# One-hot factors of the PEER gate matrix: built for 12 tokens at once in bf16, with the gate in three bf16 parts

## The chip, the cores and the metric

The kernel runs on one core of one Trainium2 chip. The metric is the device time of one execution in microseconds (us), as the median over runs; lower is better. Three runs of the kernel before gave 2867.94, 2873.04 and 2873.58 us.

## The reference

The program is a whole two-layer model in fp32 on 512 tokens of width 1024: a mixing layer (HGRN2 and retention branches), a PEER feed-forward layer, and a second block with recurrent, stick-breaking and differential attention and a gated feed-forward. Only the PEER layer is touched here. It retrieves, for each token and each of 8 heads, 16 of 16384 experts, and adds their outputs:

```python
s = jnp.einsum('thpd,hpkd->thpk', q, sub_keys.astype(jnp.float32))
top_s, top_i = lax.top_k(s, PEER_TOPK)
cand = top_s[:, :, 0, :, None] + top_s[:, :, 1, None, :]
cand_idx = top_i[:, :, 0, :, None] * PEER_NKEYS + top_i[:, :, 1, None, :]
...
gates = jax.nn.softmax(best_s, axis=-1)
...
act = jax.nn.gelu(jnp.einsum('td,thkd->thk', xb, u).astype(jnp.float32))
w = (gb * act).astype(xb.dtype)
return jnp.einsum('thk,thkd->td', w, v)
```

An expert's number is 128·i + j, with i and j below 128. So the gates of one token can be written as a 128x128 matrix G with G[j, i] the summed gate of expert (i, j): the product of a matrix of 128 selections by a one-hot of j, and one of 128 selections by a one-hot of i scaled with the gate.

## The kernel before

For tokens 0 to 383 (`SD = 384`, three tiles of 128) the kernel doesn't gather experts. It computes the activation of all 16384 experts densely, builds G for every token, and multiplies. For tokens 384 to 511 it gathers the rows of the chosen experts by indirect DMA, a fixed number per step (`gathers`, function `gath`); VectorE takes a product and sum of each gathered tile (line 1050, tile `junk`).

The dense part goes in steps. A step `u_step` (line 795) handles 256 experts. `begin` fetches the weights of later steps (SyncE's queue) and writes their high parts (`whi`, ScalarE, line 74). Then come the callbacks: `early`, `finish_split` (the low parts `wlo`, VectorE, line 79), `pre` (gathers and selection work), two `u_block`s on TensorE (line 779; 8 x 3 matmuls of 384 columns each, lines 58 to 60), `mid`, two GELUs on ScalarE with the store of the result (lines 819, 821), and `post`.

In 32 of these steps (12 tokens each, `TS = 12`) G is built as well; I call them gate steps.

- `g_pre` (line 995), called in `early`: for each token it makes two fp32 tiles of 128x128. J is a one-hot of j. For 11 of the 12 tokens ScalarE makes it in two passes, `Abs(iota - j)` (line 1005) and `Relu(1 - .)` (line 1011); for one token VectorE does it (line 1003). I is the one-hot of i times the gate, one VectorE instruction a token (line 1006). The per-token numbers are columns of `iT`, `jT`, `gT`, which hold the transposed indices and gates with selections on the partitions.
- `g_mid` (line 1014), called in `mid`: one fp32 matmul a token (line 1019) into `sx`, four tokens in a bank of PSUM.
- `g_post` (line 1023), called in `post`: ScalarE copies four tokens into `gst` with the token innermost, 16 tokens apart (line 1029), and a DMA stores every 16 tokens (line 1031).

`transposes` (line 896) makes `iT`, `jT` and `gT` of one 128-token tile: three TensorE transposes (line 904) and three ScalarE copies (line 906). It is called at the end of `mid`, so those copies stand ahead of the step's GELUs in ScalarE's order. It acts three times.

The order of the work on each engine is that in which the code issues it (`manual_schedule`); a step's TensorE work is: 48 matmuls of 384 columns, then the step's gate matmuls. The tiles J and I have twelve buffers for twelve tokens, so those of a step reuse the buffers that the step before read.

Of the kernel before, what the change touches and what calls it, by code (L numbers as in the profile page):

```python
# [7 lines left out]
F32 = mybir.dt.float32  # L8
BF16 = mybir.dt.bfloat16
# [3 lines left out]
AF = mybir.ActivationFunctionType  # L13
ALU = mybir.AluOpType
# [3 lines left out]
P = 128  # L18
S = 512
NT = S // P  # L20
D = 1024
# [6 lines left out]
TS = 12  # L28
# [3 lines left out]
ND = 3  # L32
# [675 lines left out]
def peer(c):  # L708
    nc, d, W = c.nc, c.d, c.W
# [3 lines left out]
    def pool(name, **kw):  # L713
        cm[name], p = c.open(name, **kw)
        return p
# [8 lines left out]
    keep = pool("p_keep")  # L724
# [9 lines left out]
        close("p_n")  # L734
    gb = pool("p_gb", bufs=2)
    gc = pool("p_gc")
    iT = gc.tile([P, ND, P], F32, name="iT")
    jT = gc.tile([P, ND, P], F32, name="jT")
    gT = gc.tile([P, ND, P], F32, name="gT")
    iota = gc.tile([P, P], F32, name="iota")  # L740
    nc.scalar.dma_start(iota, d["c_iota"])
    se = pool("p_se", bufs=2, side="right")
    s1 = pool("p_s1", side="right")
    TV = s1.tile([P, NT, 4, 16], F32, name="TV")
# [142 lines left out]
    def finish(t):  # L887
        if t < ND:
            trans.append((2, t))
        else:  # L890
            ij = IJ[t].rearrange("p u a b -> p u (a b)")
            nc.vector.scalar_tensor_tensor(gI, ij[:, 0], float(P), ij[:, 1], op0=ALU.mult, op1=ALU.add)
            ready.add(t)

    def transposes():
        if trans:
            k, t = trans.pop(0)
            if k:
                trans.insert(0, (k - 1, t))
                return  # L900
            ij = IJ[t].rearrange("p u a b -> p u (a b)")
            pt = tr.tile([P, 3, P], F32, tag="tr", name="tr")
            for u, src in enumerate((ij[:, 0], ij[:, 1], ge[:, t].rearrange("p a b -> p (a b)"))):
                nc.tensor.transpose(pt[:, u, :], src, c.ident)
            for u, (dst, sgn) in enumerate(((iT, 1.0), (jT, -1.0), (gT, 1.0))):
                nc.scalar.activation(dst[:, t, :], pt[:, u, :], AF.Copy, scale=sgn)
            ready.add(t)

    def halves(sc, t, hp):
# [62 lines left out]

    IJ, wide = {}, {}

# [9 lines left out]
    def fold(t, u):  # L984
        oh = wide[t, u]
        if u == 0:
            IJ[t] = se.tile([P, 2, 8, 16], F32, tag="ij", name="ij")
        for n in (8, 4, 2):
            nc.vector.tensor_add(oh[:, :, :, :n], oh[:, :, :, :n], oh[:, :, :, n:2 * n])
        nc.vector.tensor_add(IJ[t][:, u], oh[:, :, :, 0], oh[:, :, :, 1])  # L990

    stage = [None]
    NJ = 1

    def g_pre(t0):
        IJ = []
        for tt in range(t0, t0 + TS):
            t, u = divmod(tt, P)
            J = gb.tile([P, P], F32, tag="J", bufs=TS, name="J")
            I = gb.tile([P, P], F32, tag="I", bufs=TS, name="I")  # L1000
            lone = (tt - t0) % 4 == 3 and (tt - t0) // 4 < NJ
            if lone:
                nc.vector.tensor_scalar(J, iota, jT[:, t, u:u + 1], 0.0, op0=ALU.add, op1=ALU.is_equal)
            else:
                nc.scalar.activation(J, iota, AF.Abs, bias=jT[:, t, u:u + 1])  # L1005
            nc.vector.tensor_scalar(I, iota, iT[:, t, u:u + 1], gT[:, t, u:u + 1],
                                    op0=ALU.is_equal, op1=ALU.mult)
            IJ.append((I, J))
            if len(IJ) % 4 == 0:
                for _, J in IJ[-4:len(IJ) - 1 if lone else None]:  # L1010
                    nc.scalar.activation(J, J, AF.Relu, bias=1.0, scale=-1.0)
        return IJ

    def g_mid(IJ):
        pgs = []
        for q in range(0, TS, 4):
            pg = sx.tile([P, 4, P], F32, tag="sx", name="sx")
            for u in range(4):
                nc.tensor.matmul(pg[:, u, :], IJ[q + u][1], IJ[q + u][0], start=True, stop=True)
            pgs.append(pg)  # L1020
        return pgs

# [10 lines left out]
    def gather(table, n):  # L1033
        rows = keep.tile([P, D], F32, tag="rows", bufs=4, name="rows")
        nc.gpsimd.indirect_dma_start(out=rows, out_offset=None, in_=table,  # L1035
                                     in_offset=bass.IndirectOffsetOnAxis(ap=gI[:, n:n + 1], axis=0))
        return rows

    def gath():
        q = []  # L1040
        for n in range(2 * P + 4 - 1):
            if n < 2 * P:
                q.append(gather(d["expert_u"] if n < P else d["expert_v"], n % P))
            if n < 4 - 1:
                continue
            m = n - 4 + 1
            rows = q[m]
            if m < P:
                junk = keep.tile([P, D], F32, tag="junk", bufs=2, name="junk")
                nc.vector.scalar_tensor_tensor(junk, rows, 1.0, hG, op0=ALU.mult, op1=ALU.mult,  # L1050
                                               accum_out=gA[:, m:m + 1])
                if m == P - 1:
                    nc.scalar.activation(gA, gA, AF.Gelu_apprx_tanh)
                    nc.vector.tensor_mul(gG, gG, gA)
            else:
                g = gG[:, m - P:m - P + 1]
                if m == P:
                    nc.vector.tensor_scalar(hG, rows, g, None, op0=ALU.mult)
                else:
                    o = c.xs[:, ND, :] if m % 2 else hG  # L1060
                    nc.vector.scalar_tensor_tensor(o, rows, g, o, op0=ALU.mult, op1=ALU.add)  # L1061
                if m == 2 * P - 1:
                    nc.vector.tensor_add(c.xs[:, ND, :], c.xs[:, ND, :], hG)
            done[0] += 1
            yield 1
# [10 lines left out]
    n = 1  # L1076
# [29 lines left out]
    def v_weight(k):  # L1106
        p = vsteps[k]
        a = acts[p // 2][:, 2 * (p % 2):2 * (p % 2) + 2, :]
        whi = vg[0].tile([P, 2, SD], F32R, tag="Whi", name="Whi")
        wlo = vg[0].tile([P, 2, SD], F32R, tag="Wlo", name="Wlo")  # L1110
        gv = Gt[p // 4].rearrange("p b i t -> p i b t")[:, 2 * (p % 4):2 * (p % 4) + 2]
        av = a.rearrange("p i (b t) -> p i b t", t=TB)
        nc.vector.tensor_mul(av, av, gv)
        nc.scalar.copy(whi, a)
        nc.vector.tensor_sub(wlo, a, whi)
        wt[k] = (whi, wlo)
# [10 lines left out]
    while order[n][0] == "u":  # L1127
        st = {}
        p = order[n][1]
        go = toks < SD and (toks + TS - 1) // P in ready  # L1130

        def early():
            if go:
                st["IJ"] = g_pre(toks)
            elif vg[0] is not None:
                if not wt and order[n + 2][0] == "v":
                    v_weight(0)
            else:
                work(1.5)

        def pre():
            if ND in ready:
                gathers(RATE_W if first or rest else RATE_G if go else RATE_U)
            work(1.5 if ND in ready else 3)

        def mid():
            if go:
                st["pg"] = g_mid(st["IJ"])
            transposes()

        def post():
            if go:
                g_post(toks, st["pg"])
        if len(ready) == NT and res[0] is None:
            close("p_s1", "p_se")
            if c.second:
                b_tables(c)
            res[0] = pool("p_res", side="right")
        u_step(n, p, early, pre, mid, post)
        if go:  # L1160
            toks += TS
        elif toks >= SD and vg[0] is None and order[n + 4][0] == "v":
            close("p_gc", "p_gb", "p_ub")
            vg[0] = pool("v_g", bufs=2)
            for k in range(4):
                v_fetch(k)
        n += 1
# [5 lines left out]
    for k in range(64):  # L1173
        begin(n)
        if k + 4 < 64:
            v_fetch(k + 4)
        if k + 1 < 64:
            v_weight(k + 1)
        w = finish_split(n)
        n += 1  # L1180
        gathers(RATE_V)
        if c.second and k == 50:
            wr = keep.tile([P, D], F32, tag="junk", bufs=2, name="row_final")
            row_load(c, wr, "final_norm_w")
        if k < 62:
            for j in range(2):
                for t in range(ND):
                    prods(k, j, t, w)
        elif k == 62:
            w62 = w  # L1190
# [168 lines left out]
def second(c, out):  # L1359
# [273 lines left out]
    def project(n):  # L1633
# [13 lines left out]
        else:  # L1647
            dv = tmaj(2304)
    sq = sk = sv = dq = dk = dv = None
    st = pxt[:, 1]  # L1650
    ops = dict(X=project, I=lru1, J=lru2, K=lru3, M=lru4, A=stick_a, B=stick_b, C=stick_c, D=stick_d, a=diff_a, b=diff_b,
               c=diff_c, d=diff_d, e=diff_e, Y=y_proj, S=splits, T=diff_T, t=lambda t: run(tile_t(0, t)),
# [258 lines left out]
```

## Time and profile before

| what | value |
|---|---|
| median of 3 runs (lowest to highest) | 2873.04 us (2867.94 to 2873.58) |
| span of the profiled execution | 2869.7 us |
| TensorE matmul (PE) busy | 2792.8 us, 97% |
| TensorE weight load (PEld) busy | 2454.2 us, 86% |
| VectorE (DVE) busy | 1876.6 us, 65% |
| ScalarE (ACT) busy | 1249.2 us, 44% |
| GpSimd (POOL) busy | 427.3 us, 15% |

The profiled execution comes with its span alone, from its first instruction to its last; no time around it is given, and the span lies 3.3 us below the median of the runs. The shares are means over the whole program, which has stages with different limits. The gate steps lie between 1197 and 1573 us of the span, an eighth of it, and what the change does has to be read there.

### The profile page before, as it was taken

How to read it: one execution, taken by the hardware profiler on the slowest of the kernel's cores; microseconds unless marked ns; L12 is line 12 of the kernel's file. 1: busy time of each engine (PE TensorE's matmuls, PEld its weight loads, DVE VectorE, ACT ScalarE, POOL GpSimd, SP SyncE). 2: the span in 40 equal slices, each digit the busy share in tenths (PEclk: the TensorE clock that was granted, in tenths of full speed). 3: DMA queues.
4: the chain of work that ended last, by engine and by line, in shares of the span. 5: the costliest groups of instructions: out<-in, count | busy, mean ns of one | idle time of the engine just before them, and what ended most of it. 6: DMA issues, size and time to landing. Idle time of an engine off the chain costs nothing.

```text
span 2869.7 us, 40522 instructions
## 1 busy us (share of the span) xinstructions
PE 2792.8 (97%) x15905; PEld 2454.2 (86%) x15905; DVE 1876.6 (65%) x3717; ACT 1249.2 (44%) x2110; POOL 427.3 (15%) x333
## 2 busy tenths in 40 slices
PE   8999999999999999999999999999999999999998
PEld 7888888988989889999999988888887766888988
DVE  4666434345453999967777677777777568575475
ACT  4222223322233325689999333333334676432232
POOL 0000011011000002323332433232331020010010
PEclk9999999999999999999999999999999999999999
DMA  4111222222233237889999889999993210322222
GB/s 144 69 65 59 74 96 78 92 83 77 77 118 96 100 107 263 280 305 324 334 325 331 319 296 330 334 333 336 340 347 131 83 59 30 82 91 89 100 86 77
DMA packets 177679, 499.18 MB, mean 174 GB/s; under 512 B 46288, under 2 KB 96080, under 8 KB 144208
## 3 DMA queue, kind: packets, MB, share of 16 engines
q1 hardware_dynamic: 94416, 311.16, 30.8%
q0 software_dynamic: 36864, 134.23, 13.2%
q10 hardware_dynamic: 46208, 51.18, 5.1%
q8 instruction: 126, 2.06, 0.3%
q14 instruction: 65, 0.53, 0.1%
HBM read 448.83 MB, written 47.71 MB: 173 GB/s over the span
## 4 chain that ended last, share of the span: by engine, by line
PE 76%; DVE 8%; ACT 7%; issue 4%; DMA 3%; ACTq 1%; POOL 1%; DVEq 0%; POOLq 0%
PE mm L58 15%; PE mm L60 15%; PE mm L59 15%; PE acc L60 6%; PE acc L59 6%; PE acc L58 6%; DMA rows<-expert_u,gI 2%; ACT J L1005 2%; PE ax L385 1%; ACT gst L1029 1%; ACT whi L74 1%; DVE wlo L79 1%; PE ax L59 1%; PE ax L58 1%; PE ax L60 1%
## 5 line engine op out<-in xcount | busy, mean ns | idle before, releaser
L79 DVE TENSOR_TENSOR wlo<-wraw,whi 128x2048 fp32r<-128x2048 f32 (+1 forms) x250 | 561.6, 2246 | 394.5 <-ACT whi L74 382.8
L58 PE MATMUL mm<-hh,whi 128*128 128x512 f32 (+2 forms) x2064 | 755.9, 366 | 14.1 <-ACT hh L244 7.3
L74 ACT CAST whi<-wraw 128x2048 fp32r<-128x2048 f32 (+1 forms) x250 | 468.7, 1875 | 683.9 <-PE acc L60 305.9
L60 PE MATMUL mm<-hh,wlo 128*128 128x512 f32 (+2 forms) x2064 | 747.3, 362 | 8.8 <-DVE wlo L79 8.3
L59 PE MATMUL mm<-hl,whi 128*128 128x512 f32 (+2 forms) x2064 | 748.3, 363 | 0.3
L58 PEld LDWEIGHTS mm<-hh,whi 128*128 128x128 f32 x2064 | 390.7, 189 | 57.6 <-ACT hh L244 8.4
L60 PEld LDWEIGHTS mm<-hh,wlo 128*128 128x128 f32 x2064 | 390.4, 189 | 53.1 <-DVE wlo L79 11.6
L59 PEld LDWEIGHTS mm<-hl,whi 128*128 128x128 f32 x2064 | 390.5, 189 | 41.7 <-DVE hl L245 1.1
L59 PE MATMUL acc<-wlo,Whi 128*128 128x512 f32 x768 | 304.6, 397 | 0.1
L58 PE MATMUL acc<-whi,Whi 128*128 128x512 f32 x768 | 304.5, 397 | 0.0
L60 PE MATMUL acc<-whi,Wlo 128*128 128x512 f32 x768 | 304.5, 396 | 0.0
L1035 POOL DMA_INDIRECT rows<-expert_u,gI x128 | 158.5, 1239 | 743.6 <-issue 417.9
L58 PE MATMUL mm<-whi,hh 128*128 128x256 f32 x888 | 249.5, 281 | 0.3 <-ACT hh L244 0.3
L60 PE MATMUL mm<-whi,hl 128*128 128x256 f32 x888 | 248.8, 280 | 0.8 <-DVE hl L245 0.8
L59 PE MATMUL mm<-wlo,hh 128*128 128x256 f32 x888 | 249.1, 281 | 0.0
L1035 POOL DMA_INDIRECT rows<-expert_v,gI x128 | 179.2, 1400 | 380.0 <-DVE xs L1061 179.7
L59 PEld LDWEIGHTS acc<-wlo,Whi 128*128 128x128 f32 x768 | 144.7, 188 | 35.7 <-DVE wlo L79 0.6
L60 PEld LDWEIGHTS acc<-whi,Wlo 128*128 128x128 f32 x768 | 144.6, 188 | 35.2
L58 PEld LDWEIGHTS acc<-whi,Whi 128*128 128x128 f32 x768 | 144.7, 188 | 35.2
L58 PEld LDWEIGHTS mm<-whi,hh 128*128 128x128 f32 x888 | 166.7, 188 | 2.9 <-issue 1.4
L60 PEld LDWEIGHTS mm<-whi,hl 128*128 128x128 f32 x888 | 166.6, 188 | 1.8 <-DVE hl L245 1.3
L59 PEld LDWEIGHTS mm<-wlo,hh 128*128 128x128 f32 x888 | 166.5, 187 | 1.2 <-issue 0.8
(501 smaller groups left out, 4285.6 us busy)
## 6 DMA issues: line engine op xcount, KB each, us to landing
wraw<-expert_ut SPq DMA_DIRECT2D x64, 1024.0 KB, 5.5
wraw<-expert_vt SPq DMA_DIRECT2D x64, 1024.0 KB, 6.6
wraw<-w_in SPq DMA_DIRECT2D x58, 1024.0 KB, 4.8
s_G<-gst ACTq DMA_DIRECT2D x24, 1024.0 KB, 8.4
Gt<-s_G SPq DMA_DIRECT2D x16, 1536.0 KB, 13.1
wraw<-w_ff_up SPq DMA_DIRECT2D x22, 1024.0 KB, 4.8
s_act<-act ACTq DMA_DIRECT2D x52, 384.0 KB, 6.2
at<-s_act SPq DMA_DIRECT2D x26, 768.0 KB, 12.3
```

What stands on the lines that cost most here:

```text
L58: nc.tensor.matmul(out, lh, rh, start=start, stop=False)
L59: nc.tensor.matmul(out, lh, rl, start=False, stop=False)
L60: nc.tensor.matmul(out, ll, rh, start=False, stop=stop)
L74: self.c.nc.scalar.copy(hi, raw)
L79: self.c.nc.vector.tensor_sub(lo, raw, hi)
L385: nc.tensor.matmul(ps[:m, t], kp[:, t * P:t * P + m], qt[:, t, :, 1, :], start=True, stop=True)
L1005: nc.scalar.activation(J, iota, AF.Abs, bias=jT[:, t, u:u + 1])
L1029: nc.scalar.copy(stage[0][:, :, o:o + 4].rearrange("p i t -> p t i"), pg)
L1035: nc.gpsimd.indirect_dma_start(out=rows, out_offset=None, in_=table, in_offset=bass.IndirectOffsetOnAxis(ap=gI[:, n:n + 1], axis=0))
```

## The change

J and I become tiles for 12 tokens each, bf16, with the token innermost: element (k, t) lies 12 elements of 2 bytes from (k+1, t). `grid` holds the number k at every (k, t) and is written once. VectorE compares `grid` with the 12 columns of `jT` or `iT`, spread over k, in one instruction each. The gate is split into three bf16 parts that add up to it exactly (`gT[:, 0]` to `gT[:, 2]`); three multiplications give three I tiles, the last in place. A step whose 12 tokens lie in two tiles of 128 does each of these five in two pieces (2 of the 32). Per token, three bf16 matmuls add into the place of the one fp32 matmul. ScalarE makes no J any more. `transposes` moves from `mid` to `post`, after the GELUs, and gains three VectorE instructions for the split. To make room, `junk` has one buffer instead of two.

```diff
-    iT = gc.tile([P, ND, P], F32, name="iT")
-    jT = gc.tile([P, ND, P], F32, name="jT")
-    gT = gc.tile([P, ND, P], F32, name="gT")
+    iT = gc.tile([P, ND, P], BF16, name="iT")
+    jT = gc.tile([P, ND, P], BF16, name="jT")
+    gT = gc.tile([P, 3, ND, P], BF16, name="gT")
     iota = gc.tile([P, P], F32, name="iota")
     nc.scalar.dma_start(iota, d["c_iota"])
+    grid = gc.tile([P, P, TS], BF16, name="grid")
+    nc.vector.tensor_copy(grid, iota[:, :, None].to_broadcast([P, P, TS]))
...
-            for u, (dst, sgn) in enumerate(((iT, 1.0), (jT, -1.0), (gT, 1.0))):
-                nc.scalar.activation(dst[:, t, :], pt[:, u, :], AF.Copy, scale=sgn)
+            nc.scalar.copy(iT[:, t, :], pt[:, 0, :])
+            nc.scalar.copy(jT[:, t, :], pt[:, 1, :])
+            nc.scalar.copy(gT[:, 0, t, :], pt[:, 2, :])
+            left = gc.tile([P, P], F32, name="left")
+            nc.vector.tensor_sub(left, pt[:, 2, :], gT[:, 0, t, :])
+            nc.vector.tensor_copy(gT[:, 1, t, :], left)
+            nc.vector.tensor_sub(gT[:, 2, t, :], left, gT[:, 1, t, :])
...
     def g_pre(t0):
-        IJ = []
-        for tt in range(t0, t0 + TS):
-            t, u = divmod(tt, P)
-            J = gb.tile([P, P], F32, tag="J", bufs=TS, name="J")
-            I = gb.tile([P, P], F32, tag="I", bufs=TS, name="I")
...
-        return IJ
-
-    def g_mid(IJ):
+        J = gb.tile([P, P, TS], BF16, tag="J", bufs=1, name="J")
+        I = [gb.tile([P, P, TS], BF16, tag=f"I{e}", bufs=1, name=f"I{e}") for e in range(3)]
+        for dst, src in ((J, jT), (I[0], iT)):
+            for sl, t, us, shape in runs(t0):
+                nc.vector.tensor_tensor(dst[:, :, sl], grid[:, :, sl], src[:, t, None, us].to_broadcast(shape),
+                                        op=ALU.is_equal)
+        for e in (2, 1, 0):
+            for sl, t, us, shape in runs(t0):
+                nc.vector.tensor_mul(I[e][:, :, sl], I[0][:, :, sl], gT[:, e, t, None, us].to_broadcast(shape))
+        return J, I
+
+    def g_mid(JI):
+        J, I = JI
         pgs = []
         for q in range(0, TS, 4):
             pg = sx.tile([P, 4, P], F32, tag="sx", name="sx")
             for u in range(4):
-                nc.tensor.matmul(pg[:, u, :], IJ[q + u][1], IJ[q + u][0], start=True, stop=True)
+                for e in range(3):
+                    nc.tensor.matmul(pg[:, u, :], J[:, :, q + u], I[e][:, :, q + u], start=e == 0, stop=e == 2)
             pgs.append(pg)
         return pgs
...
-                junk = keep.tile([P, D], F32, tag="junk", bufs=2, name="junk")
+                junk = keep.tile([P, D], F32, tag="junk", bufs=1, name="junk")
...
         def mid():
             if go:
                 st["pg"] = g_mid(st["IJ"])
+
+        def post():
             transposes()
-
-        def post():
             if go:
                 g_post(toks, st["pg"])
```

How this moves the instructions of a gate step. First TensorE, at the end of a step's large matmuls. Before, one row stands for the twelve fp32 products between the last matmul of a step and the first of the next:

```order
L60 MATMUL mm<-hh,wlo 128x384
L1019 MATMUL sx<-I,J 128x128 x12
L58 MATMUL mm<-hh,whi 128x384
L59 MATMUL mm<-hl,whi 128x384
L60 MATMUL mm<-hh,wlo 128x384
```

In the changed kernel (I_10593 is the first of the three I tiles, I_10594 the second, I_10595 the third):

```order
L60 MATMUL mm<-hh,wlo 128x384
L1028 LDWEIGHTS J
L1028 MATMUL sx<-I_10593,J 128x128
L1028 LDWEIGHTS J
L1028 MATMUL sx<-I_10594,J 128x128
L1028 LDWEIGHTS J
L1028 MATMUL sx<-I_10595,J 128x128
L1028 LDWEIGHTS J
L1028 MATMUL sx<-I_10593,J 128x128
```

Where twelve products stood, 36 stand, each with a weight load of J of its own.

Second VectorE in the same step, between the split of the weights of one step and the next. Before:

```order
L1050 SCALAR_TENSOR_TENSOR junk,gA<-rows,hx 128x1024 x3
L1006 TENSOR_SCALAR I<-iota,iT,gT 128x128 x3
L1003 TENSOR_SCALAR J<-iota,jT 128x128
L1006 TENSOR_SCALAR I<-iota,iT,gT 128x128 x9
L79 TENSOR_TENSOR wlo<-wraw,whi 128x2048
```

Now:

```order
L1059 SCALAR_TENSOR_TENSOR junk,gA<-rows,hx 128x1024 x3
L1014 TENSOR_TENSOR J<-grid,jT 128x1536
L1014 TENSOR_TENSOR I_10838<-grid,iT 128x1536
L1018 TENSOR_TENSOR I_10840<-I_10838,gT 128x1536
L1018 TENSOR_TENSOR I_10839<-I_10838,gT 128x1536
L1018 TENSOR_TENSOR I_10838<-I_10838,gT 128x1536
L79 TENSOR_TENSOR wlo<-wraw,whi 128x2048
```

Five large instructions take the place of thirteen small ones, in the same place.

Third ScalarE, from the split of a weight to the copies of G, in the step in which the last tile's transposes are made. Before:

```order
L74 CAST whi<-wraw 128x2048
L1005 ACTIVATE J<-iota,jT 128x128 x3
L1011 ACTIVATE J<-J 128x128 x3
L1005 ACTIVATE J<-iota,jT 128x128 x4
L1011 ACTIVATE J<-J 128x128 x4
L1005 ACTIVATE J<-iota,jT 128x128 x4
L1011 ACTIVATE J<-J 128x128 x4
L906 ACTIVATE iT<-tr 128x128
L906 ACTIVATE jT<-tr 128x128
L906 ACTIVATE gT<-tr 128x128
L819 ACTIVATE act<-mm 128x384 x2
L821 DMA s_act<-act 128x768
```

Now:

```order
L74 CAST whi<-wraw 128x2048
L821 ACTIVATE act<-mm 128x384 x2
L823 DMA s_act<-act 128x768
L907 CAST iT<-tr 128x128
L908 CAST jT<-tr 128x128
L909 CAST gT<-tr 128x128
L1038 COPY gst<-sx 128x4x128 x2
```

The 22 instructions for J are gone, and the copies of the transposes stand behind the GELUs and the store.

## Rows read from the trace of the kernel before

**Rows 1.** The page, parts 1 and 2: busy time by engine; GB/s by slice.
```profile
PE 2792.8 (97%) x15905; PEld 2454.2 (86%) x15905; DVE 1876.6 (65%) x3717; ACT 1249.2 (44%) x2110; POOL 427.3 (15%) x333
...
GB/s 144 69 65 59 74 96 78 92 83 77 77 118 96 100 107 263 280 305 324 334 325 331 319 296 330 334 333 336 340 347 131 83 59 30 82 91 89 100 86 77
```

**Rows 2.** Busy time by stretch: all gate steps, then one; header names the columns.
```profile
core 0: us, PE busy (x) PEld busy (x) DVE busy (x) ACT busy (x) POOL busy (x), PEclk, DMA share, GB/s
1197.10:1572.60 375.50, 365.40 (x2307) 360.77 (x2307) 288.77 (x638) 345.33 (x897) 110.63 (x94) 0.99 0.89 320
1371.90:1383.60 11.70, 11.35 (x73) 11.16 (x72) 9.00 (x21) 10.85 (x29) 3.56 (x3) 1.00 0.95 346
```

**Rows 3.** The chain of work within 1240 to 1300 us, shares by line.
```profile
by line: ACT J L1005 24.9%; ACT gst L1029 20.2%; ACT whi L74 18.5%; ACT J L1011 15.4%; PE sx L1019 6.1%; issue 5.6%; ACT act L819 5.0%; ACTq L1031 2.2%; ACTq L821 2.2%; ACTq L1355 0.7%; ACTq L1029 0.1%; ACTq L74 0.0%
```

**Rows 4.** Waits of PE in the gate steps: us in total, times, longest us.
```profile
PE sx L1019 <- ACT J L1011: 9.0, 20, 2.6
PE mm L58 <- ACT act L819: 2.2, 2, 1.1
```

**Rows 5.** Timeline of PE, one gate step: start us, duration us, instruction, count.
```profile
1360.88 2.84 PE L1019 MATMUL sx<-I,J 128*128 128x128 f32 x24
1363.50 0.45 PE L58 MATMUL mm<-hh,whi 128*128 128x384 f32 x1
...
1371.93 1.95 PE L1019 MATMUL sx<-I,J 128*128 128x128 f32 x16
1374.23 1.16 PE L1019 MATMUL sx<-I,J 128*128 128x128 f32 x8 [0.35 <-ACT J L1011]
1375.20 0.44 PE L58 MATMUL mm<-hh,whi 128*128 128x384 f32 x1
```

**Rows 6.** Groups of ACT, 900 to 1600 us: busy us, mean ns | idle before.
```profile
L1005 ACT ACTIVATE J<-iota,jT 128x128 f32<-128x128 f32 x352 | 113.2, 397 | 0.0
...
L1011 ACT ACTIVATE J<-J 128x128 f32<-128x128 f32 x352 | 80.2, 302 | 0.0
```

**Rows 7.** Groups of DVE, 900 to 1600 us: same columns.
```profile
L1050 DVE SCALAR_TENSOR_TENSOR junk<-rows,hx 128x1024 f32<-128x1024 f32 x122 | 143.2, 1220 | 1.4 <-DMA rows<-expert_u,gI 1.4
L1006 DVE TENSOR_SCALAR I<-iota,iT,gT 128x128 f32<-128x128 f32 x384 | 108.1, 362 | 1.5 <-PE sx L1019 1.5
...
L982 DVE TENSOR_TENSOR wide<-wide,TI 128x2048 bf16<-128x2048 bf16 x8 | 9.8, 1225 | 0.3
L981 DVE TENSOR_TENSOR wide<-wide,iota 128x2048 bf16<-128x2048 bf16 x8 | 9.8, 1220 | 0.0
...
L990 DVE TENSOR_TENSOR ij<-wide 128x128 f32<-128x128 bf16 x8 | 3.3, 410 | 0.3
L942 DVE TENSOR_TENSOR cd<-TV 128x48 f32<-128x48 f32 x16 | 3.2, 202 | 0.0
L942 DVE TENSOR_TENSOR cd<-TV 128x16 f32<-128x16 f32 x16 | 2.7, 169 | 0.0
```

**Rows 8.** Timeline of DVE, one gate step; in brackets idle time before, releaser.
```profile
1363.35 1.03 DVE L1006 TENSOR_SCALAR I<-iota,iT,gT 128x128 f32<-128x128 f32 x3
...
1364.36 2.38 DVE L1006 TENSOR_SCALAR I<-iota,iT,gT 128x128 f32<-128x128 f32 x9
1369.39 2.29 DVE L79 TENSOR_TENSOR wlo<-wraw,whi 128x2048 fp32r<-128x2048 f32 x1 [2.65 <-ACT whi L74]
1371.60 1.22 DVE L1050 SCALAR_TENSOR_TENSOR junk<-rows,hx 128x1024 f32<-128x1024 f32 x1
...
1375.04 1.03 DVE L1006 TENSOR_SCALAR I<-iota,iT,gT 128x128 f32<-128x128 f32 x3
```

**Rows 9.** Timeline of ACT: two strided copies of G; two plain ones elsewhere.
```profile
1365.73 1.92 ACT L1029 COPY gst<-sx 128x512 f32<-128x512 f32 x2 [0.45 <-ACT gst L1029]
...
474.25 1.09 ACT L244 ACTIVATE roh<-tr 128x512 fp32r<-128x512 f32 x2
```

**Rows 10.** Timeline of PE, matmuls of 256 columns.
```profile
2689.84 0.28 PE L59 MATMUL ax<-wlo,ah 128*128 128x256 f32 x1
2689.96 0.28 PE L60 MATMUL ax<-whi,al 128*128 128x256 f32 x1
```

**Rows 11.** Timeline of PE, the first matmul behind a tile's transposes.
```profile
1153.79 0.44 PE L58 MATMUL mm<-hh,whi 128*128 128x384 f32 x1 [1.09 <-ACT act L819]
```

More of the change, by code (lines that the diff above doesn't have):

```diff
@@ L992, in peer, with runs @@
     stage = [None]
-    NJ = 1
-    def g_pre(t0):
-        IJ = []
-        for tt in range(t0, t0 + TS):
-            t, u = divmod(tt, P)
-            J = gb.tile([P, P], F32, tag="J", bufs=TS, name="J")
-            I = gb.tile([P, P], F32, tag="I", bufs=TS, name="I")
[L1001 to L1011, printed above, removed]
-        return IJ
-    def g_mid(IJ):
+    def runs(t0):
+        n = 0
+        while n < TS:
+            t, u = divmod(t0 + n, P)
+            m = min(TS - n, P - u)
+            yield slice(n, n + m), t, slice(u, u + m), [P, P, m]
+            n += m
+    def g_pre(t0):
+        J = gb.tile([P, P, TS], BF16, tag="J", bufs=1, name="J")
[10 more added lines that the diff above has]
+        J, I = JI
         pgs = []
@@ L1182, in peer @@
         if c.second and k == 50:
-            wr = keep.tile([P, D], F32, tag="junk", bufs=2, name="row_final")
+            wr = keep.tile([P, D], F32, tag="junk", bufs=1, name="row_final")
             row_load(c, wr, "final_norm_w")
```

## The prediction

> **What bounds the kernel now.** The page comes first: PE is busy for 97% of the span and ACT for 44% [rows 1]. That is a mean over stages, so the next view is busy time by stretch. The 32 gate steps take 375.5 us, 11.73 us each; in one of them ACT is busy for 10.85 of 11.70 us and PE for 11.35 [rows 2]. To see which of two nearly full engines sets the pace I read the chain of work inside the stretch. It runs over ACT: the two passes that make J hold 24.9% + 15.4% of it, and the gate products on PE 6.1% [rows 3]. The waits agree. PE stands 20 times for a J, 9.0 us in all [rows 4]; in the timeline of a step such a wait is the 0.35 us ahead of the last 8 records [rows 5]. So in a gate step PE has about 11 us of work and ACT makes it 11.7.
>
> The same timeline gives PE's part. The 48 large matmuls run from 1363.50 to 1371.93, that is 8.43 us. An undisturbed gate group runs from 1360.88 to 1363.50: 24 records, two for each of 12 fp32 products, in 2.62 us, or 0.109 us a record [rows 5]. Together 11.05 us. [...]
>
> **The change, part by part.** I write p for the time from one bf16 product to the next. All that PE does in a step is then 8.43 + 36p, and the question is whether anything else takes longer.
>
> *ACT.* 11 + 11 instructions a step go (352 of each in 32 steps, 397 and 302 ns [rows 6]; (113.2 + 80.2) / 32 = 6.0 us a step). ACT falls from 10.85 to about 4.8 us and is no bound any more. The waits for J go with it, as does the work that was lost after the longest one, 2.6 us [rows 4].
>
> *DVE.* Thirteen small instructions go: 1363.35 to 1364.36 + 2.38 = 1366.74, so 3.39 us a step [rows 8]. Five come. The nearest rows are the compare and the product of the selection work, also bf16 with one operand spread over an inner run: 2048 elements in 1.22 us [rows 7]. For 1536 I take three quarters, 0.92 us; the inner run is 12 long there and 16 here, so 1.22 is the other bound. 5 x 0.92 = 4.6 us. With the weight split (1369.39 to 1371.60, 2.21) and three gathered rows (1371.60 to 1375.04, 3.44 [rows 8]) DVE has 10.25 us a step. J has one buffer, so its first compare waits for the last product of the step before. Behind it in DVE's queue stands `wlo` of the next step, due 12 us later; 4.6 + 2.21 fit. DVE is covered as long as PE's step is over 10.25 us; without that cover it costs the difference. The two steps in two pieces cost five more instruction starts each; at most the whole 0.17 us of a 16-element add apiece [rows 7], and covered too.
>
> *Small parts.* `grid` (one conversion of 1536 elements) and the split of the gate (three small DVE instructions, three times) stand in DVE's queue beside the large matmuls of a step whose weights were split a step earlier: nothing. Without that cover they would cost 1.7 us (1536 elements at 1.03 ns [rows 7], plus a start) and about 1 us a tile. One buffer for `junk`: its users follow each other on DVE alone; nothing. Moving `transposes` behind the GELUs frees the first matmul of the next step, which waits 1.09 us for a GELU behind the copies [rows 11]; of three such waits two lie outside the stretch: -2.2 us. POOL, SP and the stores are issued as before.
>
> *PE, the term that decides.* 36 products of 128 columns, each with its own weight load, take the place of 24 records. Both operands are read with 24 bytes between neighbours, and no matmul here has that, nor bf16. The bounds:
>
> - Lowest: reading apart costs nothing. Matmuls of 256 columns start every 0.12 us (2689.84 to 2689.96 [rows 10]), so half of it, p = 0.060.
> - Reading apart costs the engine twice its time. DVE reads single bf16 values 32 bytes apart in the last fold: 410 ns for 128. The plain adds cost (202 - 169) / 32 = 1.03 ns an element, so 128 would take 202 + 80 x 1.03 = 284; the difference is 0.98 ns an element, which doubles it [rows 7]. ACT, writing 64 bytes apart, needs 1.92 us for two copies of 512 against 1.09 plain: 1.76 times [rows 9]. For PE twice 0.060 is 0.120; the records of this very shape come every 0.109 today [rows 5]. I take 0.115.
> - Highest: the cost is a time, not a factor. Adding ACT's (1.92 - 1.09) / 1024 = 0.81 ns or DVE's 0.98 ns to 0.467 ns a column gives p = 0.164 to 0.186; DVE's whole 2.0 ns an element gives 0.257.
>
> A row for DVE's reads of the same type with a like distance stands nearest, and it says "double", in that engine's own cycle.
>
> [...]
>
> *The sum.* PE's step becomes 8.43 + 36 x 0.115 = 12.57 us; 32 of them 402.2 against 375.5: +26.7. Less 2.2: +24.5 us. The profiled span goes from 2869.7 to 2894; it lay 3.3 below the median of the runs, so 2897 us there. With p from 0.109 to 0.125 the steps are 12.35 to 12.93 us and the time 2891 to 2909. The decision lies at 8.43 + 36p = 375.5 / 32 + 2.2 / 32, p = 0.094.
>
> **Rival A, faster: the distance costs PE little.** One mechanism on PE alone, decided at p = 0.094. For it: weight loads and matmuls are two streams (PEld beside PE [rows 1]) and the fp32 operands of today are twice as wide, so a bf16 stream has room. Against it: two engines pay for distance. At p = 0.060 a step is 10.59 us. DVE's 10.25 stays below, but the transfers may not: a step moves 320 GB/s x 11.73 us = 3.75 MB [rows 2], and the highest rate of any slice is 347 GB/s [rows 1], so 10.8 us. 32 x 10.8 = 346: -29.5 - 2.2, or 2841 us.
>
> [...]
>
> **Rival C, much slower: the distance costs a fixed time.** With p = 0.164 to 0.257 a step is 14.3 to 17.7 us and the time 2953 to 3061. For it: ACT's and DVE's extra per element are near each other (0.81 and 0.98 ns), as if the memory and not the engine set them. [...]
>
> **Rival D: the change doesn't do what it says on DVE.** If the five instructions run at the 1.03 ns an element of the plain fp32 adds, each takes about 1.7 us, DVE's step is 5.65 + 8.5 = 14.2 us, and the time 2950. Against it: 2048 elements in 1.22 us [rows 7] are twice as fast, with the same operations, type and spreading.
>
> **How the numbers follow.** The forecast (distance doubles PE's time) has 0.38, A 0.26, C 0.30, D and the rest 0.06. A measurement of this kernel tells 0.2%, some 6 us, from no change. A is faster by more than that in nearly all of its cases (0.25); the others are slower; between them, with p close to 0.094, some 0.05: faster 0.25, same 0.05, slower 0.70. The range has to take in most of A and the lower two thirds of C: 2838 to 3015, which leaves out about 0.05 and 0.12. The forecast's own range is 2891 to 2909.
>
> **What would show it.** In the profile after: ACT in a gate step near 5 us; the five DVE instructions near 0.9 us; no wait of PE for J; the chain of the stretch on PE; and 36 matmuls of line 1028 in 4.1 us between a step's last large matmul and the next step's first. If that group takes 2 to 3 us, A holds, and then DMA or DVE ends the chain. If it takes 6 us and more, C. If PE waits ahead of the group for DVE, D. The forecast is wrong if p lies outside 0.10 to 0.13, or if the time moves in a stretch other than 1150 to 1575 us.

## The result, and the profile after

The changed kernel takes 3084.36 us (median of four runs, 3080.41 to 3086.71), beside 2873.31 (2867.94 to 2874.43) for the kernel before on the same chip. The ratio is 1.0733, 95% interval 1.072 to 1.0746: 211 us slower. The forecast was 2897 us, range 2838 to 3015. The sign was right, the change was nearly nine times the one forecast, and the time lies outside the range and even above the dearest case of rival C.

The page of the changed kernel, parts 1, 2 and 5, against [rows 1] (part 5: line, engine, operation, out<-in, count | busy us, mean ns | idle before):

```profile
span 3084.9 us, 39981 instructions
...
PE 3021.4 (98%) x16289; PEld 2585.7 (84%) x16289; DVE 1924.9 (62%) x3481; ACT 1090.5 (35%) x1406; POOL 427.5 (14%) x333
...
PEclk9999999999999999778777799999999899999999
...
GB/s 146 57 69 55 85 103 69 86 83 82 97 115 93 101 268 260 209 198 210 214 211 209 198 260 319 320 333 339 335 319 322 91 71 40 63 87 88 99 86 79
...
L1028 PE MATMUL sx<-I,J 128*128 128x128 bf16 x1152 | 274.2, 413 | 0.0
```

ACT fell from 44% to 35% of the span, as meant. PE rose to 98%. Two things were not in the forecast: in the slices of the gate steps the granted clock is down to 7 and 8 tenths, and the transfers run at some 210 GB/s where they ran at 320 [rows 2]. The mean of 413 ns in the last line is the length of one modelled record, which overlaps the next; the pace has to be read from the starts, below.

Busy time by stretch, changed kernel: all gate steps, one step (product group to product group), and that step cut where the granted clock changes.

```profile
core 0: us, PE busy (x) PEld busy (x) DVE busy (x) ACT busy (x) POOL busy (x), PEclk, DMA share, GB/s
1198.40:1785.80 587.40, 587.40 (x2694) 485.57 (x2693) 335.96 (x402) 189.21 (x198) 118.15 (x96) 0.78 0.59 208
1391.41:1409.54 18.13, 18.13 (x86) 14.94 (x85) 9.73 (x13) 5.87 (x6) 3.10 (x3) 0.81 0.61 212
1391.41:1395.92 4.51, 4.51 (x21) 2.87 (x21) 0.36 (x2) 1.54 (x2) 1.90 (x2) 1.00 1.01 345
1395.93:1402.75 6.82, 6.82 (x28) 5.43 (x27) 2.68 (x3) 3.77 (x3) 0.00 (x0) 0.50 0.69 270
1402.76:1409.54 6.78, 6.78 (x41) 6.62 (x39) 6.68 (x9) 0.55 (x2) 1.20 (x1) 1.00 0.25 64
```

The stretch of 375.50 us [rows 2] became 587.40: +211.9, of 215.2 between the two profiled spans (3084.9 and 2869.7). PE is busy in every microsecond of it, and the waits view shows no wait of PE at all between 1150 and 1800 us; the 9.0 us for J [rows 4] are gone. So nothing is late: PE itself has more to do, or does it more slowly. The timeline of PE in that step says which (start us, duration us, instruction, count):

```profile
1391.41 8.59 PE L1028 MATMUL sx<-I,J 128*128 128x128 bf16 x36
1399.63 0.69 PE L58 MATMUL mm<-hh,whi 128*128 128x384 f32 x1
1400.12 0.52 PE L59 MATMUL mm<-hl,whi 128*128 128x384 f32 x1
1400.44 0.52 PE L60 MATMUL mm<-hh,wlo 128*128 128x384 f32 x1
...
1402.36 0.52 PE L60 MATMUL mm<-hh,wlo 128*128 128x384 f32 x1
1402.68 0.38 PE L58 MATMUL mm<-hh,whi 128*128 128x384 f32 x1
1402.90 0.34 PE L59 MATMUL mm<-hl,whi 128*128 128x384 f32 x1
1403.07 0.34 PE L60 MATMUL mm<-hh,wlo 128*128 128x384 f32 x1
```

Two things stand here. The 36 products run from 1391.41 to 1399.63, p = 8.22 / 36 = 0.228 us, 0.2325 as the median between two starts; forecast was 0.115. And the large matmuls behind them start every 0.32 us until 1402.68 and every 0.175 after it, which is where the granted clock goes from 0.50 back to 1.00. The products don't feel that change: it falls at 1395.93, in the middle of the group, and they start every 0.233 us before it and every 0.231 after it.

Over 32 steps: the products take 36 x 0.2325 = 8.37 us a step where 4.14 were forecast, +135 us. The mean step is 587.4 / 32 = 18.36 us; less 8.43 and 8.37 there remain 1.56 us, +50 us. They are the half clock's: 256 us of the stretch are at a granted clock of 0.50, 6.8 before. Counted over the stretch in the trace, 1144 starts of one large matmul after another at the full clock lie 0.175 us apart and 328 at the half clock 0.335, in the mean; 328 x 0.16 is 52 us. With the 24.5 of the forecast the three make 210, of 211 measured.

DVE did what was forecast. Its groups, 1190 to 1800 us, and its wait in the same stretch (waits view: us in total, times, longest):

```profile
L1018 DVE TENSOR_TENSOR I<-I,gT 128x1536 bf16<-128x1536 bf16 x90 | 83.6, 956 | 2.1
L1014 DVE TENSOR_TENSOR J<-grid,jT 128x1536 bf16<-128x1536 bf16 x30 | 28.7, 956 | 210.9 <-PE sx L1028 210.9
L1014 DVE TENSOR_TENSOR I<-grid,iT 128x1536 bf16<-128x1536 bf16 x30 | 28.5, 951 | 0.0
```

```profile
DVE J L1014 <- PE sx L1028: 226.6, 30, 8.6
```

0.956 us an instruction against 0.92. Its first compare waits for the last product, as forecast, some 210 to 227 us in all by the two views; PE never waits in turn, so this wait costs nothing.

### The profile page after: what moved, and what is told of

It is laid out like the page before. It is cut to its first block, busy times and chain, and to the rows that moved or that the text cites. A ratio compares the mean times of both kernels' runs of the same rounds, so it can differ in the third digit from the quotient of the medians.

```text
span 3084.9 us, 39981 instructions
## 1 busy us (share of the span) xinstructions
PE 3021.4 (98%) x16289; PEld 2585.7 (84%) x16289; DVE 1924.9 (62%) x3481; ACT 1090.5 (35%) x1406; POOL 427.5 (14%) x333
## 4 chain that ended last, share of the span: by engine, by line
PE 67%; issue 19%; DVE 7%; POOL 3%; ACT 2%; DMA 1%; ACTq 1%; SPq 0%; POOLq 0%; DVEq 0%
PE mm L60 14%; PE mm L58 14%; PE mm L59 14%; PE acc L59 5%; PE acc L60 5%; PE acc L58 5%; POOL rows L1044 3%; DVE wlo L79 1%; PE ax L385 1%; PE ax L59 1%; PE ax L58 1%; PE ax L60 1%; PE ax L467 1%; PE ax L559 1%; DVE mr L671 0%
## 5 line engine op out<-in xcount | busy, mean ns | idle before, releaser
L58 PE MATMUL mm<-hh,whi 128*128 128x512 f32 (+2 forms) x2064 | 782.1, 379 | 11.1 <-ACT hh L244 7.3
L60 PE MATMUL mm<-hh,wlo 128*128 128x512 f32 (+2 forms) x2064 | 769.6, 373 | 9.0 <-DVE wlo L79 8.5
L59 PE MATMUL mm<-hl,whi 128*128 128x512 f32 (+2 forms) x2064 | 770.5, 373 | 0.3
L58 PEld LDWEIGHTS mm<-hh,whi 128*128 128x128 f32 x2064 | 411.5, 199 | 56.4 <-ACT hh L244 8.4
L60 PEld LDWEIGHTS mm<-hh,wlo 128*128 128x128 f32 x2064 | 407.7, 198 | 53.8 <-DVE wlo L79 12.2
L59 PEld LDWEIGHTS mm<-hl,whi 128*128 128x128 f32 x2064 | 408.7, 198 | 41.7 <-DVE hl L245 1.4
L1028 PE MATMUL sx<-I,J 128*128 128x128 bf16 x1152 | 274.2, 413 | 0.0
L1028 PEld LDWEIGHTS <-J 128*128 128x128 bf16 x1152 | 164.5, 146 | 99.0 <-issue 4.0
L1014 DVE TENSOR_TENSOR J<-grid,jT 128x1536 bf16<-128x1536 bf16 (+2 forms) x34 | 30.7, 909 | 226.6 <-PE sx L1028 226.6
```

Source lines behind the costliest of these rows:

```text
L58: nc.tensor.matmul(out, lh, rh, start=start, stop=False)
L59: nc.tensor.matmul(out, lh, rl, start=False, stop=False)
L60: nc.tensor.matmul(out, ll, rh, start=False, stop=stop)
L1014: nc.vector.tensor_tensor(dst[:, :, sl], grid[:, :, sl], src[:, t, None, us].to_broadcast(shape), op=ALU.is_equal)
L1028: nc.tensor.matmul(pg[:, u, :], J[:, :, q + u], I[e][:, :, q + u], start=e == 0, stop=e == 2)
```

## The experiments

Two questions: what of the doubled p is due to the distance between neighbours in memory, and on which operand; and whether the lost clock is a cost of its own. The operand that is loaded as weights is J, the one that streams past it is I.

**e1: both operands adjacent.** The same 36 products, each on 128 neighbouring columns. If the distance is what costs, p falls to the 0.060 of the lowest bound and the time toward rival A's.

```diff
-                    nc.tensor.matmul(pg[:, u, :], J[:, :, q + u], I[e][:, :, q + u], start=e == 0, stop=e == 2)
+                    at = slice((q + u) * P, (q + u + 1) * P)
+                    near = [x.rearrange("p k t -> p (k t)")[:, at] for x in (J, I[e])]
+                    nc.tensor.matmul(pg[:, u, :], near[0], near[1], start=e == 0, stop=e == 2)
```

> Edit: the 36 products of a gate step read 128 adjacent elements of J and of each I tile instead of every twelfth; everything else, VectorE's work included, stays. G is then wrong in its values. [...] Rival R1 (bf16 products with a weight load each, or three adding into one place, cost this whatever they read): a product still takes 0.23 us and the time stays near 3084 us.

Measured: 2836.86 us (two runs), ratio 0.9872 (0.9852 to 0.9891). Timeline of PE, then the stretch of the gate steps (columns as above):

```profile
1404.13 2.18 PE L1030 MATMUL sx<-I,J 128*128 128x128 bf16 x36
1406.12 0.42 PE L58 MATMUL mm<-hh,whi 128*128 128x384 f32 x1
```

```profile
1196.90:1543.00 346.10, 340.73 (x2694) 333.99 (x2693) 330.16 (x397) 183.53 (x198) 131.10 (x93) 0.99 0.94 344
```

The group takes 1.99 us, p = 0.056, and the clock stays at 0.99. All of the loss hangs on how the operands lie: read adjacent, the same 36 products make the change a gain of 37 us.

**e2 and e3: one operand at a time.** In e2 J is read adjacent and I 24 bytes apart, in e3 the other way round. The edit of e2, against e1's line:

```diff
-                    nc.tensor.matmul(pg[:, u, :], near[0], near[1], start=e == 0, stop=e == 2)
+                    nc.tensor.matmul(pg[:, u, :], near[0], I[e][:, :, q + u], start=e == 0, stop=e == 2)
```

> Edit: J (loaded as weights) is read adjacent, the I tiles (the moving operand) every twelfth element as in the changed kernel. G is wrong in its values. Theory T-moving (the moving read sets the pace): 0.23 us a product and 3070 to 3090 us. Rival T-weights (the weight load sets it): 0.06 to 0.08 us a product and 2835 to 2870 us. If both pay: something between.

> Edit: J is read every twelfth element, the I tiles adjacent. G is wrong in its values. T-moving: 0.06 to 0.08 us a product and 2835 to 2870 us. T-weights: 0.23 us and 3070 to 3090 us. If both streams pay alike side by side: 0.23 us in this run and in the run with only the moving operand apart.

Measured: e2 3078.5 us, e3 2840.84, one run each. Timeline of PE and the stretch, of e2:

```profile
1406.25 8.35 PE L1030 MATMUL sx<-I,J 128*128 128x128 bf16 x36
1414.24 0.68 PE L58 MATMUL mm<-hh,whi 128*128 128x384 f32 x1
```

```profile
1198.30:1778.10 579.80, 579.80 (x2694) 457.24 (x2693) 335.97 (x402) 188.26 (x198) 118.15 (x96) 0.79 0.60 211
```

and of e3:

```profile
1401.46 2.39 PE L1030 MATMUL sx<-I,J 128*128 128x128 bf16 x36
1403.66 0.42 PE L58 MATMUL mm<-hh,whi 128*128 128x384 f32 x1
```

```profile
1198.60:1542.30 343.70, 341.97 (x2695) 336.28 (x2694) 331.53 (x399) 185.04 (x198) 130.07 (x94) 1.00 0.94 348
```

As the median between two starts e2 has 0.227 us, e3 0.060. It is the streamed operand, nearly alone; weights 24 bytes apart cost 4 ns a product. The clock goes the same way: 0.79 in e2, 1.00 in e3.

**e4: the changed kernel with groups of 4 tokens.** The tiles are built as three groups of [128, 4], so that neighbours are 8 bytes apart and two of them share 16 bytes. DVE's instructions stay as many and as large (`grid` becomes [128, 128, 4] and is read three times over).

```diff
-        J = gb.tile([P, P, TS], BF16, tag="J", bufs=1, name="J")
+        J = gb.tile([P, TS // TG, P, TG], BF16, tag="J", bufs=1, name="J")
...
-                    nc.tensor.matmul(pg[:, u, :], J[:, :, q + u], I[e][:, :, q + u], start=e == 0, stop=e == 2)
+                    at = (q + u) // TG, slice(None), (q + u) % TG
+                    nc.tensor.matmul(pg[:, u, :], J[(slice(None), *at)], I[e][(slice(None), *at)], start=e == 0, stop=e == 2)
```

> Edit: J, the I tiles and grid lie in groups of 4 tokens, token innermost, so that neighbours are 8 bytes apart instead of 24; the same five VectorE instructions a step (inner run 4 instead of 12). If the cost is one per 16-byte line touched (0.2325 us for 128 lines), 64 lines cost about 0.117 us: step 8.43 + 4.2 = 12.6 us, 2895 to 2910 us. [...] VectorE: 0.96 us an instruction as now, unless the short inner run slows it (up to 1.7 us, then VectorE sets the step at 14 us).

Measured: 2899.82 us, ratio 1.009 (1.0073 to 1.0107); p = 0.118, a step 12.64 us.

```profile
1408.66 4.43 PE L1033 MATMUL sx<-I,J 128*128 128x128 bf16 x36
1412.84 0.43 PE L59 MATMUL mm<-hh,whi 128*128 128x384 f32 x1
```

```profile
1197.80:1602.40 404.60, 404.60 (x2694) 397.60 (x2693) 335.86 (x402) 191.22 (x198) 120.50 (x96) 1.00 0.85 299
```

At a third of the distance p halves, and the clock stays at 1.00. It also tests the forecast's arithmetic by accident: with p = 0.118 the formula 8.43 + 36p gives 12.68 us a step, and 12.64 were measured.

**e5: groups of 2 tokens.** The edit of e4 with TG = 2: four bytes apart, four neighbours in 16 bytes.

> Edit: as with groups of 4, with groups of 2 tokens: neighbours 4 bytes apart, 32 lines of 16 bytes for 128 elements. If a product costs 1.82 ns a line touched, as 128 lines (0.2325 us) and 64 lines (0.118 us) did, 32 lines cost 0.058 us, near the 0.056 us of adjacent reads: step 10.5 to 10.8 us, 2835 to 2850 us, 0.8 to 1.3% faster than the kernel before. [...]

Measured: 2836.67 us (2834.43 to 2839.24), ratio 0.9871 (0.9856 to 0.9886), p = 0.057. This is the version that beats both kernels, by 37 and 248 us, with the same computation.

```profile
1399.41 2.24 PE L1033 MATMUL sx<-I,J 128*128 128x128 bf16 x36
1401.46 0.42 PE L59 MATMUL mm<-hh,whi 128*128 128x384 f32 x1
```

```profile
1195.90:1538.90 343.00, 338.91 (x2694) 332.29 (x2693) 330.09 (x397) 184.25 (x198) 127.75 (x93) 1.00 0.95 347
```

It is as quick as adjacent reading (e1). PE, DVE (330 of 343 us) and the transfers (share 0.95) are now all nearly full. In the waits of PE ahead of the products, 1150 to 1600 us, DVE's multiplication has taken ACT's place, but for 2.3 us where the kernel before had 9.0; other waits come to 2.4:

```profile
PE sx L1033 <- DVE I L1022: 2.3, 3, 1.1
```

**e7: three distances in one group.** The streamed operand is read 8 elements (16 bytes) apart in the first twelve products, 6 (12 bytes) in the next, 2 (4 bytes) in the last; J stays 24 bytes apart.

```diff
-                    nc.tensor.matmul(pg[:, u, :], J[:, :, q + u], I[e][:, :, q + u], start=e == 0, stop=e == 2)
+                    step = {0: 8, 4: 6, 8: 2}[q]
+                    apart = I[e].rearrange("p k t -> p (k t)")[:, u:u + step * P:step]
+                    nc.tensor.matmul(pg[:, u, :], J[:, :, q + u], apart, start=e == 0, stop=e == 2)
```

> Edit: the changed kernel, with the I tiles read every 8th element in the first bank of four tokens (16 bytes apart, 128 lines), every 6th in the second (12 bytes, 96 lines), every 2nd in the third (4 bytes, 32 lines). G is wrong in its values. Theory (1.82 ns a line): 0.233, 0.175 and 0.058 us a product. Rival (cost in proportion to the distance, 0.2325 us at 24 bytes): 0.155, 0.116 and 0.056 us. [...]

Measured: 2984.7 us, one run. In the group below, the twelve starts of the first kind run from 1387.445 to 1390.031 (0.233 apart, the median), of the second from 1390.263 to 1392.222 (0.178), of the third from 1392.398 to 1393.467, 0.06 to 0.08 at first and 0.107 after that: at 1392.57 the granted clock had gone to half.

```profile
1387.44 6.33 PE L1030 MATMUL sx<-I,J 128*128 128x128 bf16 x36
```

By stretch, for the tile `sx` alone: one line for each kind (the counts take in matmuls that began before the stretch; the second line leaves out the first start of its kind).

```profile
core 0: us, PE busy (x) PEld busy (x) ACT busy (x), PEclk, DMA share, GB/s
1387.43:1390.25 2.82, 2.81 (x12) 0.00 (x0) 0.00 (x0) 1.00 0.87 336
1390.42:1392.38 1.96, 1.96 (x13) 0.00 (x0) 1.06 (x1) 1.00 0.77 270
1392.38:1393.75 1.37, 1.37 (x14) 0.00 (x0) 1.05 (x1) 0.57 0.80 248
```

So 16 bytes apart costs as much as 24, and 12 bytes less than either. A price in proportion to the distance is excluded; one that follows the number of 16-byte pieces touched fits (128, 128 and 96 of them). Of the products only the quick ones slow down at the half clock: 0.107 us at clock 0.50, where the adjacent ones of e1 take 0.056 at 1.00; 128 columns in 0.107 us are 1.2 a ns, as are 384 in the 0.32 us of the large matmuls at 0.50.

**e6: the products in three blocks.** Twelve products each, between large matmuls, as a test of whether the clock falls because the slow products stand together; if it does, a step should gain by their being spread.

```diff
+            if k in (1, 4):
+                part()
...
+        def part():
+            if go:
+                if "gen" not in st:
+                    st["gen"], st["pg"] = g_mid(st["IJ"]), []
+                st["pg"].append(next(st["gen"]))
+
         def mid():
-            if go:
-                st["pg"] = g_mid(st["IJ"])
+            part()
```

`g_mid` now pauses after every twelve products, and `part` issues the next twelve; it is called twice among the large matmuls of the second half of a step, and once behind them.

> Edit: the changed kernel with its 36 products in three blocks of 12 (2.8 us each) among the large matmuls of the second half of the step, instead of one block of 8.4 us; same instructions, same reads. [...]

Measured: 3096.08 us, one run; not less time, but 12 us more than the changed kernel (the four runs of the changed kernel lie within 6 us). In the stretch:

```profile
1200.60:1796.00 595.40, 593.46 (x2662) 483.82 (x2662) 329.67 (x391) 181.26 (x192) 117.22 (x95) 0.87 0.56 202
```

The clock did rise, from 0.78 to 0.87 (160 us at half instead of 256), but the step grew to 18.8 us in the mean: steps without a drop took about 16.9, those with one or more 17.7 to 20.7. Over 8.43 + 36 x 0.233 = 16.82 a mean step loses 2.0 us, 63 us in all for 160 us at half clock (3.5 of them waits of PE for DVE), where the changed kernel loses 50 for 256. With the blocks spread out, the half clock falls mostly on large matmuls, which feel it (0.32 us against 0.1756 in the changed kernel): by the starts in the trace some 118 of the 160 us, against 110 of the 256 in the changed kernel, where the rest falls on slow products, which don't (0.231 against 0.233). So the clock was at half for less time, and the step didn't gain by it; what brings the clock down stays open.

**e8: the kernel before with only the transposes moved.** The one part of the change that doesn't touch the products.

```diff
-            transposes()
 
         def post():
+            transposes()
```

> Edit: the kernel before, with nothing of the change but the call of transposes behind the GELUs and the store. Expected: the three waits of 1.09 us for a GELU go, 3.3 us; the long wait for J in the fourth gate step (2.6 us and the half clock behind it) may shrink too, some 3 us more; 2864 to 2872 us, 0.1 to 0.3% faster. Rival (the later iT copies hold up J and with it PE, so the waits only move): no change.

Measured: 2870.8 us against 2873.39, ratio 0.9992 (0.9983 to 1.0001). The waits of PE, 1150 to 1600 us, were in the kernel before

```profile
PE sx L1019 <- ACT J L1011: 9.0, 20, 2.6
PE mm L58 <- ACT act L819: 3.3, 3, 1.1
```

and have lost the three for a GELU; what is left is

```profile
PE sx L1019 <- ACT J L1011: 9.2, 20, 3.0
```

The waits for a GELU go, as expected; the long wait for J doesn't shrink (3.0 us at the longest, 2.6 before). The middle of the interval is -2.3 us, where 3.3 were expected of the three waits; the interval reaches no change, so no gain in time is shown.

## Why the prediction was wrong in size

**The failed step is p,** the time from one product to the next: "Reading apart costs the engine twice its time", and with it "I take 0.115". Measured: 0.2325 us, twice that and 4.2 times the 0.056 of adjacent operands. The value came from rows of two other engines (410 against 284 ns, 1.92 against 1.09 us [rows 7, 9]) carried over as a factor. What the runs show in its place is a rate of TensorE's own. Write L for the 16-byte pieces that 128 streamed columns touch; in these runs the time grows with the distance up to 16 bytes (0.178 us at 12, 0.233 at 16) and no further (0.2325 at 24):

| streamed columns | L | us from one product to the next | ns a piece |
|---|---|---|---|
| adjacent (e1) | 16 | 0.056 | - |
| 4 bytes apart (e5) | 32 | 0.057 | - |
| 8 bytes (e4) | 64 | 0.118 | 1.84 |
| 12 bytes (e7) | 96 | 0.178 | 1.85 |
| 16 bytes (e7) | 128 | 0.233 | 1.82 |
| 24 bytes (after) | 128 | 0.2325 | 1.82 |

About 1.83 ns a piece, with a floor of 0.056 us, the time of adjacent operands (e1). 4 bytes apart is where the two meet: 32 pieces are 0.059. In e4, e5 and the changed kernel the weights lie as far apart as the streamed operand, in e7 24 bytes; with adjacent weights e2 has 0.227 for its 128 pieces.

The number could have been read from the rows quoted. The large matmuls stream four-byte columns, four to a piece: 48 of them in 8.43 us [rows 5] are 0.1756 us for 96 pieces, 1.83 ns each, and 256 columns every 0.12 us [rows 10] are 64 pieces at 1.87. I read the second row as 0.47 ns a *column* and halved it. A third width in the same trace agrees: 512 four-byte columns, 128 pieces, start every 0.233 us (nine starts in 2.10 us), the price of the slow products.

```profile
2608.85 0.39 PE L60 MATMUL mm<-hh,wlo 128*128 128x512 f32 x1
...
2610.95 0.39 PE L60 MATMUL mm<-hh,wlo 128*128 128x512 f32 x1
```

That these large matmuls are themselves held by this rate was not tested by a run; it fits that those of 384 columns take 0.1756 us at clock 1.00 and 0.32 at 0.50, which is less than twice as long (0.351). With 128 pieces at 1.83 ns, p would have been 0.234, a step 16.9 us, and the forecast some 3035 us: rival C, which had 0.30, and whose upper bound of 0.257 came from DVE's 2.0 ns an element.

Of the distances tried only 2 elements apart was free for the streamed operand (0.057 us, e5, against 0.056 adjacent, e1): 4 apart costs twice the adjacent time (0.118 us, e4) and 8 apart four times (0.233 us, e7).

**A term was missing: the clock.** The formula takes the large matmuls at 8.43 us after the change too, as they ran in a stretch with a granted clock of 0.99 [rows 2]. The clock was 0.78, and 1.56 us a step went with it, some 50 us in all; this is what carries the time beyond rival C. That it goes with the slow products is shown: 256 us of the stretch are at half in the changed kernel and 249 in e2, 160 in e6 and 103 in e7, none in e3, e4 and e5, and in e1 the same 6.8 us as in the kernel before. PE counts as busy for 100% of the stretch all the while, so its busy share gave no warning. What in the slow products brings the clock down was not found.

**The rest, point by point.** *The formula* 8.43 + 36p held where the clock stayed up (e4: 12.68 against 12.64). *ACT* is off the bound, at 189.21 / 32 = 5.9 us a step where about 4.8 was forecast. The 6.0 taken off for J was a sum of single durations, and these overlap: between 1190 and 1580 us of the kernel before, ACT's groups add up to 382 us, its busy time to 352. The miss costs nothing, as PE waits for it nowhere. *DVE* at 0.956 us an instruction and 335.96 / 32 = 10.5 us a step, forecast 0.92 and 10.25: right, and rival D is out. *J's single buffer* makes DVE wait and PE not: right. *The transposes*: the waits are gone as said; the -2.2 us for them is not shown as time (e8, -2.3 within the noise). *Rival A* was what e1, e3 and e5 show, for the other layouts: 2837 to 2841 us measured, 2841 worked out, and the transfers near full as the rival said.

## What to carry to other kernels

Before a layout is turned so that one engine can work on many items at once, look at how far apart each later reader will find its neighbours, the streamed operand of a matmul above all (0.17 us a product for 24 bytes here, e2 against e1), and price that by a rate of that same engine (here 1.83 ns a piece of 16 bytes); a factor from another engine's rows was no price here (0.115 us taken, 0.2325 measured). A middle layout may do for both: here groups of 2 left DVE's instructions as many and as long (0.950 to 0.955 us, e5, against 0.956), and gave PE back all of its speed (0.057 us a product against 0.056 adjacent). And where a part of the work becomes slow while the engine still counts as busy, look at the granted clock of what runs beside it (0.78 here, with PE busy for 100% of the stretch).

## What the hardware showed that was not expected

- The slow products of the changed kernel are paid for twice: in the step shown the granted clock is 0.50 from the middle of their group on (1395.93 to 1402.75), and the large matmuls behind them take 0.32 us instead of 0.1756. The slow ones themselves take 0.233 us before the clock falls and 0.231 after it.
- The two operands of a matmul differ: 24 bytes apart costs the streamed one 0.17 us a product (e2 against e1), the weights 4 ns (e3 against e1).
- VectorE's five instructions took the same time however the tokens were grouped: 0.956 us for 1536 elements in groups of 12, 0.96 and 0.95 in groups of 4 (e4's timeline), 0.950 to 0.955 in groups of 2 (e5).
